# The first attention loads go from GpSimd's DMA queue to SP's

## The chip, the cores and the metric

The kernel runs on one core of one Trainium2 chip. A time is the device time of one execution in microseconds. The engines are TensorE (PE, with its weight loads PEld), VectorE (DVE), ScalarE (ACT), GpSimd (POOL) and SyncE (SP). SP computes nothing; it issues DMAs, and its queue carries nearly all of them. GpSimd computes and issues DMAs too.

## The reference

Two layers of a diffusion backbone over 512 latent tokens and 256 context tokens, width 1024. Each layer is a modulated SwiGLU feed-forward, token mixing, and another feed-forward. Layer 0 mixes by a short convolution and a 2-D Fourier transform, layer 1 by differential attention (8 heads, each with two maps of 64 columns) beside latent attention (8 heads). The part that matters here is the differential head:

```python
s = jnp.einsum('bqhmd,bkhmd->bhmqk', q_da, k_da).astype(f32) * DA_SCALE
p = jax.nn.softmax(s, axis=-1)
w_diff = p[:, :, 0] - lam * p[:, :, 1]
o_da = jnp.einsum('bhqk,bkhd->bqhd', w_diff, v_da.astype(f32))
```

The 512 queries attend to 768 keys (256 of the context, 512 latent) in one softmax.

## The kernel before

All matrix products run in float32r. Where full precision is wanted, a value is split into a high and a low part, and three matmuls are added up (`mm3`, L213 to L215). Weights come in chunks of 512 KB through SP's queue (L129) into three raw buffers; ScalarE makes the high part (L141), VectorE or GpSimd the low part (L143), in four pairs of buffers.

In layer 1 the kernel first makes the projections of the attention. Each result is split into a staging tile (`stg`, four buffers) and stored to DRAM by SP: queries and keys by L727, latent values by L991, values by L845. The order of the last of these items in the program is: keys of head group 0, latent queries (first half), their rotary part, latent queries (second half), values of group 0. The rotary part computes with VectorE (L735), GpSimd (L736, L739) and ScalarE (L738), and stores four times; each half of it gives two stores. The second half of the latent queries gives two more stores. The values of group 0 come in three tiles, with two stores each.

Then the attention begins, as a generator that runs beside the projections of groups 1 to 3, so that TensorE has projection matmuls (keys of group 1 first) between the score matmuls. There are four groups, and each has the heads da 0, mla 0, da 1, mla 1. A head's data is loaded back from DRAM by `load_da` or `load_mla`: for each of the two maps of a differential head the high part of the queries (L1044), the keys (L1045) and the low part of the queries (L1046), and for both maps the values (L1049). The queries are broadcast to both halves of the partitions. All of these are DMAs that GpSimd issues. The first head's loads stand in the program at the start of the attention, behind the value projection of group 0; each later head's stand one query tile after the head before it has begun.

A query tile of a head (`da_unit`) makes scores for map 0 (L1021, four matmuls: high and low queries against 512 and 256 keys), the maximum on VectorE (L1011), the exponential on ScalarE (L1013), and the same for map 1; the difference of the two is then transposed by TensorE (L1030) and multiplied with the values (`av_da`, `st<-wt,v`).

The program's order isn't the order of an engine's queue. A scheduler puts the instructions of each engine in order ahead of the run: what is ready at that point in its own model of time, and among those what comes first in the program. On the chip each engine then takes its instructions strictly in that order, and a DMA that has to wait for a store to land holds up whatever stands behind it on the engine that issues it.

Of the kernel before, what the change touches and what calls it, by code (L numbers as in the profile page):

```python
# [10 lines left out]
F32 = mybir.dt.float32  # L11
# [65 lines left out]
class Builder:  # L77
# [958 lines left out]

    def load_da(self, g, hd):

        dma = self.nc.gpsimd.dma_start
        maps = []  # L1040
        for m in (2 * hd, 2 * hd + 1):
            q, ql, k = self.qstack(), self.qstack(), self.kstack()
            qd = self.qd[g].rearrange("h a r m t -> m h (a r) t")[m]
            dma(out=q, in_=qd[0:1].to_broadcast([2, 64, SEQ]))  # L1044
            dma(out=k, in_=self.kd[g].rearrange("h a r m t -> m (h a r) t")[m])  # L1045
            dma(out=ql, in_=qd[1:2].to_broadcast([2, 64, SEQ]))  # L1046
            maps.append((q, ql, k))
        v = self.atpool.tile([P, 3, 2, 2, P], F32R, name=self.nm("v"), tag="v", bufs=2)
        dma(out=v.rearrange("p j h i c -> p j (h i) c"), in_=self.vd[g][hd])  # L1049
        return maps, v  # L1050
# [606 lines left out]
```

## Time and profile before

| | us |
|---|---|
| median of 3 runs | 2997.54 (2997.32 to 2999.41) |
| the profiled execution | 2996.09 |
| its span | 2994.3 |
| TensorE busy | 2874.3 (96%) |
| VectorE, ScalarE, GpSimd busy | 1650.9, 1043.5, 820.5 |
| the attention's score matmuls, first and last start | 2162.7, 2546.3 |

Every view below counts microseconds from the start of the span. In an order of time, a bracket gives the idle time of the engine before the instruction and what ended it. An issue line gives the tile written, the tile read, the queue, the count, the size of one, and the median time from issue to landing. A releaser named for a wait on several things is the one that came last by the profile. TensorE's granted clock is 1.00 at the higher of its two levels, 2.4 GHz, and 0.50 at the lower, 1.2 GHz.

### The profile page before, as it was taken

The numbers are of one execution on the slowest core, as the hardware profiler recorded it, in microseconds if no ns is written. First come the engines' busy times: TensorE is split into PE (matmuls) and PEld (weight loads), VectorE is DVE, ScalarE is ACT, GpSimd is POOL, SyncE is SP. The second block draws the span as 40 slices with busy tenths as digits, with TensorE's granted clock in tenths as the row PEclk, the third lists the DMA queues.
The fourth block names the chain that finished last, engine by engine and source line by source line (L and its number), as shares of the span: only waits on it lengthen the run. The fifth ranks groups of instructions, "written<-read, shape, count | busy, mean of one in ns | idle before, by whom it ended". The sixth has DMA issues, their size and how long they took to land.

```text
span 2994.3 us, 44211 instructions
## 1 busy us (share of the span) xinstructions
PE 2874.3 (96%) x17842; PEld 2549.9 (85%) x17842; DVE 1650.9 (55%) x2966; ACT 1043.5 (35%) x1733; POOL 820.5 (27%) x441
## 2 busy tenths in 40 slices
PE   6999999999999999999999999999899999999998
PEld 5888888878878888888788888887788888899997
DVE  7866676565475433435845334366366667653335
ACT  4422121444343221124431122244344555552223
POOL 4221112423242111114311111143433332442222
PEclk9999999999999999999999999999999999999999
DMA  7754433323344322233333433352866685452334
GB/s 269 248 166 134 141 135 127 120 86 126 120 142 148 112 85 99 78 120 113 124 130 106 131 116 118 108 167 100 265 166 185 154 211 111 146 175 92 102 103 141
DMA packets 190095, 413.19 MB, mean 138 GB/s; under 512 B 58369, under 2 KB 83585, under 8 KB 189890
## 3 DMA queue, kind: packets, MB, share of 16 engines
q1 hardware_dynamic: 126930, 373.09, 37.6%
q0 software_dynamic: 62960, 37.27, 5.6%
q8 instruction: 140, 2.29, 0.3%
q14 instruction: 65, 0.53, 0.1%
HBM read 375.14 MB, written 35.00 MB: 137 GB/s over the span
## 4 chain that ended last, share of the span: by engine, by line
PE 63%; DVE 6%; DMA 3%; issue 2%; ACT 2%; POOL 2%; SPq 0%; ACTq 0%; POOLq 0%; DVEq 0%
PE mm L213 12%; PE mm L215 12%; PE mm L214 12%; PE pr L214 8%; PE pr L213 8%; PE pr L215 8%; PE pr L1021 2%; PE mm L1030 1%; ACT wh L141 1%; DVE wl L143 1%; DMA ks<-dr 1%; PE st L1115 1%; POOL wl L143 1%; DVE top L1011 1%; DMA dr<-stg 1%
## 5 line engine op out<-in xcount | busy, mean ns | idle before, releaser
L143 POOL TENSOR_TENSOR wl<-wraw,wh 128x1024 fp32r<-128x1024 f32 (+2 forms) x276 | 674.8, 2448 | 1898.1 <-ACT wh L141 1887.5
L141 ACT ACTIVATE wh<-wraw 128x1024 fp32r<-128x1024 f32 (+1 forms) x476 | 494.2, 1039 | 940.7 <-PE mm L214 577.8
L214 PE MATMUL pr<-xm,wh 128*128 128x512 f32 (+1 forms) x1760 | 635.5, 361 | 22.9 <-DVE xm L304 18.1
L213 PE MATMUL pr<-xm,wh 128*128 128x512 f32 (+1 forms) x1760 | 632.3, 360 | 8.3 <-DVE act L221 2.9
L215 PE MATMUL pr<-xm,wl 128*128 128x512 f32 (+1 forms) x1760 | 632.3, 359 | 0.0
L213 PE MATMUL mm<-xm,wh 128*128 128x256 f32 (+1 forms) x1560 | 460.1, 296 | 8.0 <-DVE xm L304 5.0
L215 PE MATMUL mm<-xm,wl 128*128 128x256 f32 (+1 forms) x1560 | 461.5, 296 | 1.8 <-DVE wl L143 1.8
L214 PE MATMUL mm<-xm,wh 128*128 128x256 f32 (+1 forms) x1560 | 460.4, 295 | 0.6 <-DVE xm L304 0.6
L213 PE MATMUL mm<-act,wh 128*128 128x256 f32 (+1 forms) x1408 | 454.1, 324 | 5.9 <-ACT y L504 2.1
L215 PE MATMUL mm<-act,wl 128*128 128x256 f32 (+1 forms) x1408 | 454.0, 323 | 2.6 <-POOL wl L143 2.6
L214 PE MATMUL mm<-act,wh 128*128 128x256 f32 (+1 forms) x1408 | 454.1, 323 | 1.5 <-DVE act L221 1.5
L214 PEld LDWEIGHTS pr<-xm,wh 128*128 128x128 f32 x1760 | 334.6, 190 | 83.5 <-DVE xm L304 27.0
L383 DVE CUSTOM_DVE_ANT_0 junk<-wmod,cond,bmod 128x1024 bf16<-128x1024 f32 x256 | 387.8, 1515 | 9.6 <-DMA wmod<-in_w_mod_dram 6.9
L213 PEld LDWEIGHTS pr<-xm,wh 128*128 128x128 f32 x1760 | 334.5, 190 | 61.4 <-DVE act L221 3.3
L215 PEld LDWEIGHTS pr<-xm,wl 128*128 128x128 f32 x1760 | 334.9, 190 | 51.2
L143 DVE TENSOR_TENSOR wl<-wraw,wh 128x1024 fp32r<-128x1024 f32 x200 | 251.5, 1257 | 210.0 <-ACT wh L141 209.5
L213 PEld LDWEIGHTS mm<-xm,wh 128*128 128x128 f32 x1560 | 295.7, 190 | 18.3 <-DVE xm L304 5.6
L215 PEld LDWEIGHTS mm<-xm,wl 128*128 128x128 f32 x1560 | 295.3, 189 | 10.2 <-DVE wl L143 2.4
L214 PEld LDWEIGHTS mm<-xm,wh 128*128 128x128 f32 x1560 | 295.3, 189 | 8.8 <-DVE xm L304 1.1
L213 PEld LDWEIGHTS mm<-act,wh 128*128 128x128 f32 x1408 | 265.3, 189 | 33.1 <-ACT act L220 3.6
L214 PEld LDWEIGHTS mm<-act,wh 128*128 128x128 f32 x1408 | 266.6, 189 | 26.2 <-DVE act L221 2.7
L215 PEld LDWEIGHTS mm<-act,wl 128*128 128x128 f32 x1408 | 265.8, 189 | 26.8 <-POOL wl L143 3.2
(240 smaller groups left out, 3445.7 us busy)
## 6 DMA issues: line engine op xcount, KB each, us to landing
wraw<-in_w_ffn_in_dram SPq DMA_DIRECT2D x250, 512.0 KB, 3.5
wmod<-in_w_mod_dram SPq DMA_DIRECT2D x160, 512.0 KB, 4.3
wraw<-in_w_ffn_out_dram SPq DMA_DIRECT2D x106, 512.0 KB, 3.6
dr<-stg SPq DMA_DIRECT2D x40, 512.0 KB, 4.7
wraw<-in_w_in_even_dram SPq DMA_DIRECT2D x32, 512.0 KB, 3.5
qs<-dr POOLq DMA_DIRECT2D x56, 256.0 KB, 11.7
dr<-stg SPq DMA_DIRECT2D x36, 256.0 KB, 6.7
ks<-dr POOLq DMA_DIRECT2D x24, 384.0 KB, 11.2
```

Of the source, the lines that this page charges most:

```text
L141: self.nc.scalar.activation(out=h, in_=r, func=AF.Copy)
L143: eng.tensor_tensor(out=l, in0=r, in1=h.bitcast(F32), op=ALU.subtract)
L213: mmul(out, w[0], x[0], start=first, stop=False)
L214: mmul(out, w[0], x[1], start=False, stop=False)
L215: mmul(out, w[1], x[0], start=False, stop=last)
L383: dot = nc.vector.tensor_tensor_reduce(out=junk, in0=w, in1=self.cond[n], op0=ALU.mult, op1=ALU.add, scale=1.0, scalar=self.bmod[:, l, row ...
L1011: nc.vector.tensor_reduce(top, ps, axis=AX.X, op=ALU.max, negate=True)
L1021: self.nc.tensor.matmul(ps[:, c0:c1], q, k[:, c0:c1], start=i == 0, stop=i == len(passes) - 1)
L1030: self.nc.tensor.transpose(ps[:, kt * P:(kt + 1) * P], w[:, (k0 + kt) * P:(k0 + kt + 1) * P], self.ident)
L1115: nc.tensor.matmul(ps, v[:, kt], wt[i][:, :, kt], start=kt == 0 and i == 0, stop=kt == 5 and i == 1)
```

## The change

In `load_da`, for the first head of group 0 alone, the seven DMAs are issued by SP instead of GpSimd. A float32r tile is written through a view as float32, since the source in DRAM is float32. Sizes, buffers and everything else stay.

```diff
     def load_da(self, g, hd):
 
+
         dma = self.nc.gpsimd.dma_start
+        if g == hd == 0:
+            dma = lambda out, in_: self.nc.sync.dma_start(out=out.bitcast(F32), in_=in_)
         maps = []
         for m in (2 * hd, 2 * hd + 1):
             q, ql, k = self.qstack(), self.qstack(), self.kstack()
```

## Rows read from the trace of the kernel before

**Rows 1.** The page of the profile: span, and busy time of TensorE (share, instructions).

```profile
span 2994.3 us, 44211 instructions
...
PE 2874.3 (96%) x17842; PEld 2549.9 (85%) x17842; DVE 1650.9 (55%) x2966; ACT 1043.5 (35%) x1733; POOL 820.5 (27%) x441
```

**Rows 2.** Table by stretch: length; PE, PEld, DVE, ACT, POOL busy; clock; DMA share; GB/s.

```profile
2160.00:2165.00 5.00, 1.04 (x6) 0.54 (x5) 1.01 (x2) 2.09 (x3) 2.50 (x4) 0.81 1.14 347
2165.00:2170.00 5.00, 3.99 (x10) 2.86 (x10) 2.09 (x2) 0.99 (x2) 2.05 (x1) 0.51 1.21 284
2170.00:2175.00 5.00, 4.07 (x19) 3.25 (x19) 2.03 (x4) 0.99 (x2) 0.00 (x0) 1.00 1.10 286
```

**Rows 3.** TensorE in order of time: start, us, instruction, [idle before and releaser].

```profile
2160.28 0.28 PE L215 MATMUL mm<-wh,xm 128*128 128x256 f32 x1
...
2162.70 0.47 PE L1021 MATMUL pr<-ks,qs 128*128 128x512 f32 x1 [2.13 <-DMA wraw<-in_w_da_q_dram]
...
2166.01 1.22 PE L1021 MATMUL pr<-ks,qs 128*128 128x512 f32 x3 [2.83 <-DMA qs<-dr]
...
2171.07 0.74 PE L1021 MATMUL pr<-ks,qs 128*128 128x512 f32 x3 [0.93 <-DMA qs<-dr]
...
2171.64 0.40 PE L213 MATMUL mm<-xm,wh 128*128 128x512 f32 x1
...
2175.14 0.86 PE L1021 MATMUL pr<-ks,qs 128*128 128x512 f32 x4
...
2175.84 0.39 PE L213 MATMUL mm<-xm,wh 128*128 128x512 f32 x1
```

**Rows 4.** GpSimd in order of time, the same columns.

```profile
2145.69 1.28 POOL L736 TENSOR_TENSOR t<-t,t 128x512 f32<-128x512 f32 x1
...
2146.91 0.84 POOL L1044 DMA_DIRECT2D qs<-dr  x1
...
2147.78 1.30 POOL L739 TENSOR_TENSOR stg<-t,stg 128x512 fp32r<-128x512 f32 x1
...
2151.75 0.87 POOL L1046 DMA_DIRECT2D qs<-dr  x1
...
2162.49 0.80 POOL L1059 DMA_DIRECT2D qs<-dr  x1 [9.30 <-DMA dr<-stg]
...
2177.70 0.58 POOL L1049 DMA_DIRECT2D v<-dr  x1 [10.65 <-DMA dr<-stg]
...
2186.01 1.29 POOL L736 TENSOR_TENSOR t<-t,t 128x512 f32<-128x512 f32 x1 [6.87 <-DVE t L735]
```

**Rows 5.** SP's DMA issues in order of time, runs of one kind merged.

```profile
2145.76 7.83 SPq L727 DMA_DIRECT2D dr<-stg  x6
...
2155.14 9.61 SPq L845 DMA_DIRECT2D dr<-stg  x4
...
2167.98 3.15 SPq L845 DMA_DIRECT2D dr<-stg  x2
```

**Rows 6.** DMA from 2140 to 2180: queues; one issue group, median us to landing.

```profile
q1 hardware_dynamic: 6022, 8.34, 64.8%
q0 software_dynamic: 6864, 3.33, 34.7%
...
v<-dr POOLq DMA_DIRECT2D x1, 768.0 KB, 4.4
```

**Rows 7.** Chain of waits, 2155 to 2200: start, us, what.

```profile
2149.59 16.37 DMA qs<-dr
```

**Rows 8.** DMA issues from 2151.6 to 2152, us to landing.

```profile
qs<-dr POOLq DMA_DIRECT2D x1, 256.0 KB, 19.3
```

**Rows 9.** DMA issues from 2145 to 2145.9, us to landing.

```profile
dr<-stg SPq DMA_DIRECT2D x1, 512.0 KB, 3.0
```

**Rows 10.** ScalarE in order of time.

```profile
2159.00 0.60 ACT L220 ACTIVATE stg<-mm 128x512 fp32r<-128x512 f32 x1 [7.37 <-DMA dr<-stg]
```

**Rows 11.** TensorE in order of time, the first product with values.

```profile
2190.58 0.28 PE L213 MATMUL st<-wt,v 128*128 128x256 f32 x1
```

## The prediction

> **What bounds the kernel now.** I read the page first: the span is 2994.3 us and TensorE is busy for 96% of it [rows 1], so the time is TensorE's work plus its gaps, and what a change at one place is worth is read from the gaps there. Next I looked for the place in a table by stretch: between 2160 and 2170 us TensorE is busy for 1.04 and 3.99 us of two stretches of 5, and the granted clock, 1.00 elsewhere, falls to 0.81 and 0.51 [rows 2]. This is the start of the attention, where the moved loads are wanted.
>
> Then TensorE's own order of time [rows 3]. The value projection of head group 0 starts its last matmul at 2160.28; its 256 columns at 2.4 GHz are 0.11 us, so TensorE could go on at about 2160.40. What stands next in its order are the scores of the first query tile. Their first matmul starts at 2162.70, the next ones at 2166.01, those of the second map at 2171.07, and from 2171.64 on the row is dense again. Between 2160.40 and 2171.64 (11.24 us) it does two groups of four score matmuls and six projection matmuls. At full clock a group of four takes 0.70 us (2175.14 to 2175.84) and a projection matmul 0.233 (fifteen from 2171.64 to 2175.14, 3.50 us): 2 x 0.70 + 6 x 0.233 = 2.80 us. So 11.24 - 2.80 = 8.4 us are lost here, the matmuls at the lower clock included.
>
> The cause is the loads. GpSimd issues the six of queries and keys from 2146.91 to 2152.6 [rows 4]. The chain of waits holds the third of them (low part of map 0's queries) for 16.37 us, from 2149.59 to 2165.96, when the scores go on [rows 7]; the sixth, issued at 2151.75, takes 19.3 us [rows 8], to 2171.05, when the second map starts. From 2140 to 2180 the 16 DMA engines have nothing free: the hardware queue takes 64.8% and the software queue 34.7% of them [rows 6].
>
> **The change part by part.** Seven DMAs (2 x query high, key, query low; 1 x value) go from GpSimd's queue to SP's, for group 0's first head alone. Nothing else is edited. The view of the queries as F32 changes no byte.
>
> (a) *GpSimd's issuing goes.* From the first to the end of the sixth are 5.7 us, less 1.3 for an L739 between them: 4.4 us [rows 4]. I count them as nothing: behind them GpSimd waits until 2162.49 for a store to land before it issues the next head's queries, so the time is hidden by that wait. The seventh, the value load, makes GpSimd wait until 2177.70 for the stores of the values; its next work starts at 2186.01 [rows 4], so nothing there either.
>
> (b) *When the loads are issued.* A moved DMA stands in SP's order, which is not the program's: on GpSimd the first load stands before the L739 instruction at 2147.78 that makes the second half of the rotary latent queries, and after the L736 at 2145.69 that belongs to the same half [rows 4], though in the program it comes after both, and after the value projection. So loads are taken as soon as they are held to be ready, at this point. On SP it lies between the stores of the first half and those of the second. SP issues six such stores from 2145.76 to 2153.59 [rows 5]. I take that place; the latest that I hold likely is right behind all six.
>
> (c) *When they land.* At 2146 the queue is short: the store issued at 2145.76 lands in 3.0 us [rows 9]. The software queue moved 3.33 MB in 34.7% of 40 us (240 GB/s at a full share), the hardware queue 8.34 MB in 64.8% (322 GB/s) [rows 6]. The six loads are 4 x 0.256 + 2 x 0.384 = 1.8 MB, 5.6 us at 322 GB/s. The store that lands in 3.0 us needs 1.6 of them for its 0.5 MB, so 1.4 us are its start and end. Behind two stores (3.3 us from 2145.8) the six are moved by 2154.7 and landed by about 2156. Behind all six stores (four more, 2.1 MB, 6.5 us from 2149.1) map 0 (0.9 MB, 2.8 us) would be there at about 2159.8 and map 1 at 2162.6. Map 0 is wanted at 2160.40 and map 1 some 2 us later, after four score and six projection matmuls. So the whole 8.4 us is open to be gained, and about 7.5 at the late place.
>
> A rule of the Trainium skill speaks against this (DMA: Bandwidth & Descriptors, section Queues, rings and completion order): each DMA engine takes turns between the rings that have work, packet by packet, so that on GpSimd's ring the loads have turns of their own, and on SP's they stand behind each store ahead. By that rule they would be slower in landing wherever more than a few stores stand ahead; at the place of (b) the trace sets only 1 MB there, and the sum stays.
>
> (d) *What comes later in exchange.* The other stores stand behind the loads now. The second value tile's evacuation waits 7.37 us on ScalarE until 2159.00 for such a store [rows 10]. The bytes up to there are the same and 1.8 MB of them move faster, so I put these landings within 2 us of now. The PSUM buffers that they hold are wanted by TensorE only some microseconds later. Cost 0, at most 2 us.
>
> (e) *The value load adds a wait to SP.* It can only go when the six value stores have landed. The last two are issued from 2167.98 to 2171.13 [rows 5], and GpSimd, which waits for the same, starts the load at 2177.70; it lands after 4.4 us [rows 6], at 2182.1. Behind it on SP then stand a weight load that nobody needs soon and the next stores, of the keys that TensorE projects in this very stretch. The first matmul that reads these values starts at 2190.58 [rows 11]; 8.4 us earlier that is 2182.2. The slack of 8.5 us is used up almost to the point: I charge 1 us, from 0 up to 5 if the value stores slip with the rest.
>
> Sum: -8.4 + 0 (d) + 1 (e) = -7.4 us, and I take -7, for the small slips that (c) and (d) leave. Later gaps of TensorE hang on its own progress (scores, softmax, transposes), so the gain moves through to the end. The profiled execution took 2996.09 us around its span of 2994.3; minus 7 that is 2989.1. The median of the runs shown is 1.45 us higher, so the forecast for the median is 2990.5. The ends of the unknown costs: -8.4 with another 2 us won by a freer DMA, about 2987; with 2 for (d) and 5 for (e) it is -1.4, about 2996.
>
> **The rivals.**
> *Given back at the values.* The gap goes, but SP's queue is longer by seven DMAs, the value stores slip by 4 to 6 us, and the value load, last in that queue, lands at 2186 to 2188 in place of 2182. TensorE then waits 4 to 6 us at its first product with values, and keeps 2 to 4 us of the gain: 2994.5. For it: SP takes 1.5 to 3 us for an issue when the queue is full (2155.14 to 2171.13 holds six value stores, one weight load and its waits [rows 5]). Against it: that time is the queue's backlog of bytes, and the bytes are no more than now.
>
> *The DMA engines are full, so nothing is won.* The Trainium skill says on the same page (section SWDGE vs HWDGE vs iDMA) that queues of different issuing engines end on the same 16 DMA engines and that another issuer saves only its issuing time. As a mechanism here: the 99.5% in [rows 6] stays, the loads land at 2163 to 2171 as now, and only GpSimd's 5 us goes, which is hidden: 2997.5. Against it: the loads are only 1.8 of 11.7 MB in these 40 us, so it is their place in line that counts, and the hardware queue moves them a third faster. I keep these two together, as they end at no measurable change.
>
> *Slower: the loads stand behind the value stores.* In the program they come after them. If SP's order keeps that, they can go only after 2171.13, when the last value store is issued [rows 5]. At 322 GB/s, behind the 0.5 MB of the last two stores, map 0 would land at about 2171.1 + 1.6 + 2.8 + 1.4 = 2176.9 and map 1 at 2179.7, against 2166 and 2171 now: 9 to 11 us later, and 1 us for more matmuls at the lower clock: 3008. It decides at one point: whether the loads' issues stand before or after the first value store (2155.14). For it: SP is busier than GpSimd, and a store earlier in the program goes first where both are ready. Against it: GpSimd's order held them ready 8 us before that store.
>
> **How the numbers follow.** The forecast gets 0.55 (its own range 2987 to 2993.5), no measurable change 0.27, slower 0.18. About 0.2%, 6 us, is what a measurement of this kernel can tell from no change; the bound is 2991.5. Of the forecast's 0.55 some 0.08 lies short of it, so faster is 0.47, the same 0.35, slower 0.18. The range of 2986 to 3002 leaves out 0.06 below and 0.13 of the slower case.
>
> **What would show it.** Right: between 2160 and 2172 TensorE has no gap over 1 us and the clock stays at 1.00; SP issues the six loads between 2146 and 2154, and they land in under 10 us; the software queue's share of 2140 to 2180 falls from 34.7% to about 15%, which leaves mainly the second head's loads. Step (e): the value load stands on SP behind the last value stores, and the first product with values starts at about 2183. Wrong: loads after 2155 on SP, a wait of the first product with values of over 3 us, or a dense stretch there whose gain is gone before the attention ends at about 2560, which would mean that the order of the later work was set by something other than TensorE.

## The result, and the profile after

The changed kernel takes 3018.68 us (median of 5 runs, 3010.09 to 3024.66) against 2997.32 of the kernel before (5 runs, 2993.23 to 2999.41): ratio 1.0074, 95% interval 1.0059 to 1.0090. It is slower by 21 us where 7 us less were forecast. The profiled execution is the slowest of the five, 3024.66 us.

The page of the changed kernel answers to [rows 1]; the last two lines are its DMA queues (packets, MB, share of 16 engines):

```profile
span 3022.9 us, 44217 instructions
...
PE 2887.3 (96%) x17842; PEld 2560.1 (85%) x17842; DVE 1650.4 (55%) x2966; ACT 1042.5 (34%) x1733; POOL 816.4 (27%) x434
...
q1 hardware_dynamic: 127882, 375.72, 37.6%
q0 software_dynamic: 58368, 34.64, 5.2%
```

The seven loads are 2.6 MB that went from the software to the hardware queue. The table by stretch, as in [rows 2] (the attention's start lies 11 us later in this execution):

```profile
2175.00:2180.00 5.00, 2.21 (x5) 1.49 (x5) 0.00 (x1) 0.00 (x0) 2.51 (x4) 0.50 0.92 191
2180.00:2185.00 5.00, 0.26 (x1) 0.00 (x0) 0.00 (x0) 0.00 (x0) 0.00 (x0) 0.50 0.73 134
2185.00:2190.00 5.00, 0.00 (x0) 0.00 (x0) 0.00 (x0) 0.00 (x0) 0.00 (x0) 0.50 0.42 120
2190.00:2200.00 10.00, 4.77 (x11) 3.41 (x12) 0.96 (x1) 0.99 (x2) 0.00 (x0) 0.50 0.59 182
```

TensorE does 7.2 us of work in 25, at the lower clock, and the other engines all but stand too. Its order of time, which answers to [rows 3]: the value projection ends at 2171.8, and the scores come at 2177.79, 2192.18 and 2199.01, each when a load has landed (for the first the bracket names none; the first key load, issued at 2167.84, takes 9.5 us).

```profile
2171.54 0.28 PE L215 MATMUL mm<-wh,xm 128*128 128x256 f32 x1
...
2177.79 0.76 PE L1021 MATMUL pr<-ks,qs 128*128 128x512 f32 x1 [5.98 <-issue]
...
2192.18 1.22 PE L1021 MATMUL pr<-ks,qs 128*128 128x512 f32 x3 [11.92 <-DMA qs<-dr]
...
2199.01 0.80 PE L1021 MATMUL pr<-ks,qs 128*128 128x512 f32 x1 [3.04 <-DMA ks<-dr]
```

SP's issues, which answer to [rows 5]:

```profile
2157.02 6.35 SPq L727 DMA_DIRECT2D dr<-stg  x6
2163.46 1.20 SPq L129 DMA_DIRECT2D wraw<-in_w_da_q_dram  x1
2164.75 1.91 SPq L845 DMA_DIRECT2D dr<-stg  x2
2166.75 1.04 SPq L1042 DMA_DIRECT2D qs<-dr  x1
2167.84 1.30 SPq L1042 DMA_DIRECT2D ks<-dr  x1
2169.24 1.34 SPq L845 DMA_DIRECT2D dr<-stg  x2
2170.64 6.79 SPq L1042 DMA_DIRECT2D qs<-dr  x2
2177.47 10.29 SPq L1042 DMA_DIRECT2D ks<-dr  x1
2187.86 0.52 SPq L129 DMA_DIRECT2D wraw<-in_w_da_q_dram  x1
2188.49 3.91 SPq L845 DMA_DIRECT2D dr<-stg  x2
2192.49 4.43 SPq L129 DMA_DIRECT2D wraw<-in_w_da_k_dram  x1
2196.97 0.50 SPq L1042 DMA_DIRECT2D qs<-dr  x1
2202.43 0.34 SPq L1042 DMA_DIRECT2D v<-dr  x1
```

Two things stand here that the prediction didn't have. The loads come after all six stores, after a weight load and after the first value tile's stores, and they are strewn among the rest: the last query load stands behind two more weight loads. And SP is held for 6.79 us by two query loads and 10.29 us by one key load. The chain of waits (the low part of map 0's queries takes from 2170.64 to 2192.14, that of map 1's from 2196.97 to 2210.29) answers to [rows 7]:

```profile
2170.64 21.50 DMA qs<-dr
...
2196.97 13.32 DMA qs<-dr
```

From 2207 to 2209 only that last load is moving (packets and MB of these 2 us, then the hardware queue's share of the 16 engines):

```profile
DMA packets 50, 0.10 MB, mean 51 GB/s; under 512 B 0, under 2 KB 0, under 8 KB 50
...
q1 hardware_dynamic: 50, 0.10, 13.2%
```

With nothing beside it, it runs at 51 GB/s on 13.2% of the engines, and 0.132 x 16 = 2.1: it has two engines of sixteen. In the middle of the gap it does not even have these to itself. GpSimd has issued the second head's loads from 2173.86 to 2177.51, and from 2184 to 2187 SP's queue is down to half of that share while most engines stand idle:

```profile
q0 software_dynamic: 132, 0.12, 15.6%
q1 hardware_dynamic: 34, 0.07, 6.9%
```

The two engines are the second cause to be tested; the place in the order is the first.

### The profile page after: what moved, and what is told of

Read it like the earlier page. It is cut to its first block, busy times and chain, and to the rows that moved or that the text cites. A ratio compares the mean times of both kernels' runs of the same rounds, so it can differ in the third digit from the quotient of the medians.

```text
span 3022.9 us, 44217 instructions
## 1 busy us (share of the span) xinstructions
PE 2887.3 (96%) x17842; PEld 2560.1 (85%) x17842; DVE 1650.4 (55%) x2966; ACT 1042.5 (34%) x1733; POOL 816.4 (27%) x434
## 4 chain that ended last, share of the span: by engine, by line
PE 64%; DVE 5%; DMA 3%; ACT 2%; issue 2%; POOL 1%; SPq 0%; ACTq 0%; DVEq 0%; POOLq 0%
PE mm L213 12%; PE mm L215 12%; PE mm L214 12%; PE pr L214 8%; PE pr L213 8%; PE pr L215 7%; PE pr L1021 2%; DMA qs<-dr 1%; PE mm L1030 1%; ACT wh L141 1%; PE st L1118 1%; POOL wl L143 1%; DMA ks<-dr 1%; DVE wl L143 1%; DVE top L1011 1%
## 5 line engine op out<-in xcount | busy, mean ns | idle before, releaser
L215 PEld LDWEIGHTS mm<-xm,wl 128*128 128x128 f32 x1560 | 295.9, 190 | 11.4 <-DVE wl L143 3.6
```

Source lines behind the costliest of these rows:

```text
L215: mmul(out, w[1], x[0], start=False, stop=last)
```

## The experiments

Totals of one kernel spread by 13 to 32 us between runs here (the kernel before: 2983 to 3015 in 29 runs of the first set), so each profile was also measured on the stretch alone: from the start of TensorE's 11,600th matmul to that of its 12,400th, the last value projection and the start of the attention. All kernels have 17,842 matmuls. The table gives this stretch in us, from one profile each.

```
kernel                         median (before beside it)  ratio, 95% interval       stretch
before                         2997.32                                               130.1
e12 before again               2995.44, one run                                      129.8
changed                        3018.68 (2997.32)          1.0074 (1.0059 to 1.0090)  152.1
e1  changed again              3024.53 (2997.57)          1.0083 (1.0051 to 1.0115)  152.8
e2  halves                     3008.80 (2997.57)          1.0032 (1.0012 to 1.0053)  137.0
e3  early                      3011.04 (2997.57)          1.0032 (1.0013 to 1.0051)  140.3
e4  early and halves           2993.11 (2997.57)          0.9981 (0.9960 to 1.0002)  123.1
e5  queries only on SP         3018.63 (2998.73)          1.0063 (1.0044 to 1.0081)  152.3
e6  keys and values only       3002.75 (2998.73)          1.0005 (0.9987 to 1.0022)  136.1
e7  halves on GpSimd           2989.85 (2998.73)          0.9972 (0.9949 to 0.9994)  122.8
e8  ScalarE's queue            3018.09 (2998.73)          1.0056 (1.0036 to 1.0076)  152.3
e9  leading 2, no copy         3007.09 (2998.36)          1.0025 (1.0005 to 1.0044)  138.9
e10 all halves, GpSimd         2985.46 (2998.36)          0.9954 (0.9938 to 0.9970)  124.5
e11 all halves, first early    2986.21 (2998.36)          0.9962 (0.9951 to 0.9973)  122.3
```

**e1, e12: the kernels again.**

> The changed kernel itself, timed beside the three kernels of this set. Two theories of the 21 us. WIDTH: a query load is written as a broadcast, its access pattern has the two copies as the outermost dimension, and on SP's hardware queue such a DMA runs on 2 of the 16 DMA engines (the slices of the changed profile that hold nothing else show a DMA share of 0.13 to 0.14 and 45 to 55 GB/s, which is two engines' worth), so 256 KB take at least 5 us, four such loads 20 us, and SP itself is held while those two rings are full. PLACE: the loads stand in SP's order among and behind the value stores and two weight loads, and this place alone makes them late. Both expect the measured time again, 3010 to 3025 us, with TensorE's gap of some 23 us net at the start of the attention.

> The kernel before, unchanged, for a second profile. The runs are compared by the stretch from the 11,600th to the 12,400th TensorE matmul (the last value projection and the attention's start), which was 130.1 us in the first profile of the kernel before and 152.1 and 152.8 in two of the changed kernel. Every theory that puts the loss into this stretch expects 129 to 131.5 again. If it is 135 or more, the stretch varies by itself and the differences of single profiles (7 us down in the halves runs) prove less.

Both as expected: 152.8 and 152.1 against 129.8 and 130.1. The stretch repeats within 0.8 us, and it holds the whole loss (22 to 23 us).

**e2: halves.** Each query load of the first head becomes two DMAs of 64 partitions (shortened; the low part likewise, and the other heads' loads stay).

```diff
-            dma(out=q, in_=qd[0:1].to_broadcast([2, 64, SEQ]))
+            for c in (slice(0, 64), slice(64, 128)):   # first head only
+                dma(out=q[c], in_=qd[0])
```

> The changed kernel, with each query load of the first head written as two DMAs of 64 partitions each (the same bytes, no broadcast), on SP as before; the place in SP's order stays much the same (first pair behind the first value tile's stores, map 1 even behind the second weight load). WIDTH: the loads run on 16 engines, land in under 8 us each, no slice of 0.13 is left, and the time is 2993 to 3002 us, the rest of the loss being the place. PLACE: the order is no better than in the changed kernel, so the time stays at 3010 to 3025.

Neither range was met: 3008.80 is between them. The stretch gives back 15 of the 22 us; 7 stay lost. So the width is most of it, and there is something beside it.

**e3: early.** The scheduler gets the first head's loads with priority.

```diff
+            if i == 0:
+                with self.tc.high_priority(2000):
+                    loads[heads[i]] = self.load_da(g, hd)
+                return
```

> The changed kernel, with the first head's loads given priority, so that they stand in SP's order between the first of the rotary part's stores and the rest of them, ahead of all value stores (the place that the prediction assumed); still broadcasts. WIDTH: four query loads of 5 us or more on the same two engines take 20 us from about 2147 on, the second map's low part lands at about 2168 to 2172, and the stores behind them are held; the time is 2996 to 3010. PLACE: the loads land before 2160 and the time is 2987 to 2993.

It is just above WIDTH's range (3011.04, 1 us over its end). The place alone gives back 12 us of the stretch and doesn't save the change. SP's order now is that of step (b): one store, then all six loads, then the other five.

```profile
2159.23 5.11 SPq L1042 DMA_DIRECT2D qs<-dr  x2
2164.39 5.66 SPq L1042 DMA_DIRECT2D ks<-dr  x1
2170.10 0.55 SPq L1042 DMA_DIRECT2D qs<-dr  x1
2170.69 10.93 SPq L727 DMA_DIRECT2D dr<-stg  x5
```

The scores hardly wait any more (1.2 us). What TensorE waits for is a buffer in PSUM, the memory it writes its results to: 13.3 us before one projection matmul, since the evacuations (the copies out of PSUM) wait for staging tiles whose stores stand behind the narrow loads. Its wait row (total, times, longest):

```profile
PE mm L213 <- DVE stg L221: 13.7, 2, 13.3
```

**e4: early and halves**, both edits.

> Both edits: loads ahead of all value stores in SP's order, and query loads as two DMAs of 64 partitions. WIDTH and PLACE together expect what the prediction expected of the change: the loads land within 10 us, no TensorE gap over 1 us between 2160 and 2172, 2987 to 2993 us. If the time is 2995 or more, something else that the prediction left out is lost at this place (the stores behind the loads, or the value load).

2993.11, 0.1 us above the range. The interval just touches no change, so the total alone shows no gain; the stretch does, with 123.1, 6.7 to 7.0 us under the kernel before. SP issues all loads between 2147.65 and 2153.7, in 0.3 to 0.6 us a DMA, and the value load at 2177.33:

```profile
2147.65 1.10 SPq L1042 DMA_DIRECT2D qs<-dr  x2
2148.81 0.57 SPq L1042 DMA_DIRECT2D ks<-dr  x1
2149.42 2.36 SPq L1042 DMA_DIRECT2D qs<-dr  x4
2151.83 0.63 SPq L1042 DMA_DIRECT2D ks<-dr  x1
2152.50 1.24 SPq L1042 DMA_DIRECT2D qs<-dr  x2
2154.78 4.28 SPq L727 DMA_DIRECT2D dr<-stg  x5
...
2177.33 0.33 SPq L1042 DMA_DIRECT2D v<-dr  x1
```

Around these scores TensorE has no gap over 0.5 us and keeps the higher clock (1.00); map 1 follows map 0 after 2.8 us, and the first product with values doesn't wait for them (rows as in [rows 3] and [rows 11]):

```profile
2161.64 0.85 PE L1021 MATMUL pr<-ks,qs 128*128 128x512 f32 x4
2164.45 0.86 PE L1021 MATMUL pr<-ks,qs 128*128 128x512 f32 x4
...
2185.34 0.28 PE L213 MATMUL st<-wt,v 128*128 128x256 f32 x1
```

**e5, e6: the change by parts.** Only the lines of the queries, or only those of keys and values, go through SP.

> Of the seven loads only the four query loads (broadcasts) go on SP's queue; keys and values stay with GpSimd. In SP's order the first two stand behind the first value tile's stores, the other two behind the second's. WIDTH: these four are what costs; 1 MB on two engines is some 20 us from about 2156 on (the shift of the early part left out), the last lands at 2176 to 2182, and the loss is 8 to 20 us: 3005 to 3018. If it were the place alone, the loss would be smaller than that of the halves run (11 us), since here none stands behind a weight load: 2998 to 3005.

> Only the two key loads and the value load go on SP's queue (128 rows outermost, all 16 engines); the query loads stay with GpSimd as broadcasts. WIDTH: no slice of 0.13, no SP issue of over 4 us; the keys come 5 to 10 us earlier than on GpSimd or not at all later, and the time is that of the kernel before, 2990 to 3002. PLACE: the keys stand behind two and four value stores, so the scores wait for them: 3003 to 3012.

The four query loads alone make the whole loss (152.3 in the stretch; 3018.63, 0.6 us above WIDTH's range). Keys and values cost nothing that the totals show, but 6 us in the stretch (a profile of the slowest of ten runs): the keys stand behind value stores, and the first scores come after a gap of 9.1 us. There PLACE was partly right, and my WIDTH range (up to 3002) was missed by 0.75.

**e8: ScalarE's queue** (shortened).

```diff
-            dma = lambda out, in_: self.nc.sync.dma_start(...)
+            dma = lambda out, in_: self.nc.scalar.dma_start(...)
```

> The seven loads as broadcasts on ScalarE's hardware queue, a ring of their own, so that nothing of SP's is ahead or behind; they stand ahead of the value evacuations in ScalarE's order. WIDTH: still two engines per query load, 20 us for four of them, with ScalarE held in its issues of 5 us or more, which delays the evacuation of the values: 3000 to 3020. PLACE: free of SP's order the loads land by 2160: 2988 to 2995.

As WIDTH expected. A hardware queue of their own, with the loads started at 2151, doesn't help: by the times of their packets the query loads never keep more than 2.1 engines busy. Now ScalarE is held in its issues and idle for 18.7 us:

```profile
2152.89 8.76 ACTq L1042 DMA_DIRECT2D qs<-dr  x2
2161.68 10.31 ACTq L1042 DMA_DIRECT2D ks<-dr  x1
2172.12 0.60 ACT L220 ACTIVATE stg<-mm 128x512 fp32r<-128x512 f32 x1 [18.70 <-issue]
```

**e9: why narrow.** The edit of e4, and a gap between the two rotary halves in DRAM (the loads that read around it are left out here).

```diff
-            dst = self.qd[g] = self.dram([2, 2, 32, 4, SEQ])
+            dst = self.qd[g] = self.dram([2, 2, 33 if g == 0 else 32, 4, SEQ])[:, :, :32]
```

> The early-halves kernel, with a gap of one row put between the two rotary halves of group 0's queries in DRAM (33 rows for 32), so that a load of 64 partitions reads 2 x 32 x 512 and its outermost dimension is 2, though nothing is read or written twice. The order on SP is the same. It tells apart why a query load is narrow: if the OUTERMOST DIMENSION sets the number of DMA engines, the eight half loads run on two engines, slices of 0.13 DMA share come back, and the start of the attention is about as slow as in the early run (17 us slower than early halves there): 3003 to 3014. If reading the same DRAM rows twice (the BROADCAST itself) was slow, this is as fast as early halves: 2987 to 2996.

The outermost dimension it is. Half loads that copy nothing twice, but read 2 x 32 x 512, bring the loss of the early run back (138.9 against 140.3, and 123.1 without the gap). From 2170 to 2172 only they move, at 51 GB/s and 13.2% again; four of them hold SP for 8.33 us, where the four of e4 take 2.36, and TensorE waits for the same PSUM buffer.

```profile
2155.94 8.33 SPq L1042 DMA_DIRECT2D qs<-dr  x4
```

```profile
PE mm L213 <- DVE stg L221: 13.2, 1, 13.2
```

**e7: the control on GpSimd**, the edit of e2 without the change.

> Control: the kernel before (all loads on GpSimd), with the first head's query loads as two DMAs of 64 partitions each. If the software queue spreads a broadcast over all 16 engines, as the steady 1.0 share of the stretch suggests, nothing is won, four more issues of 0.8 us come on GpSimd, and the time is 2994 to 3002. If it too is confined to two engines, the loads land 5 us or more earlier and the time is 2988 to 2993.

The first branch of the expectation (nothing won) was wrong and the second holds: 2989.85, and 7 us of the stretch. So these loads are narrow on the software queue too, and the kernel before shows it. From 2193 to 2195 one query load of a later head (issued at 2190.52) moves 50 packets of 2,048 B, the only ones of that size: 51 GB/s. From 2221 to 2224 two more (issued at 2214.22 and 2215.57), with what is left of a third load that is no broadcast, are all that moves, at about twice that:

```profile
DMA packets 152, 0.30 MB, mean 101 GB/s; under 512 B 4, under 2 KB 4, under 8 KB 152
q0 software_dynamic: 152, 0.30, 35.4%
```

As broadcasts (kernel before) these two land in 10.6 us, as halves (e10, below) in 4.9:

```profile
qs<-dr POOLq DMA_DIRECT2D x2, 256.0 KB, 10.6
qs<-dr POOLq DMA_DIRECT2D x4, 128.0 KB, 4.9
```

The queues differ in what several such loads do together. Here they add up: two have about 100 GB/s, and from 2351 to 2354, where only broadcasts have packets of 2,048 B, 168 of these make 115. On SP's queue two share the 51: in e5 the last two query loads are issued by 2177.97, and from 2180 to 2190 their 254 packets of 2,048 B move at 52 GB/s. So the move put onto two engines, one behind the other, what had run side by side.

A broadcast on the software queue has small packets besides. The pages of the kernel before, e7 and e10 count:

```profile
DMA packets 190095, 413.19 MB, mean 138 GB/s; under 512 B 58369, under 2 KB 83585, under 8 KB 189890
DMA packets 186575, 413.18 MB, mean 138 GB/s; under 512 B 54849, under 2 KB 80065, under 8 KB 186370
DMA packets 147856, 413.02 MB, mean 138 GB/s; under 512 B 16130, under 2 KB 41346, under 8 KB 147651
```

From the first to the second 3,520 packets go, 880 for each of the four loads, all of them under 512 B (4 B each in the trace); the data packets stay 2,048 B. How much of the 7 us is theirs and how much is the width's was not tried.

**e10, e11: all broadcasts as halves**, without and with the first head early on SP.

> The kernel before, with all query loads that were broadcasts (both kinds of heads, all groups) as two DMAs of 64 partitions each, on GpSimd. The control with the first head alone gained 7 us at the attention's start. If the software queue's small packets were also what later heads wait for, a few us more come: 2984 to 2990. If later loads are early enough anyway, it stays at 2987 to 2993; 44 more issues on GpSimd (0.55 us for a half against 0.83 for a broadcast, some 0.3 us each pair) are hidden.

> All query loads as halves; the first head's on SP ahead of the value stores, the others on GpSimd. The two gains at the attention's start are for the same gap, so they do not add: 2984 to 2992, within 4 us of the run with all halves on GpSimd.

Both within their ranges and better than both kernels: 2985.46 and 2986.21, ratios 0.9954 and 0.9962. In e10 all 48 broadcasts are halves, and 880 small packets go for each of them (third line above). The move to SP adds nothing to it that can be measured.

## Why the prediction was wrong, step by step

What bounds the kernel was read rightly: the gap at the attention's start is the loads', and filling it is worth what was worked out. (8.4 less 1 us for the values gave -7.4; e4 and e7, which fill it in two ways, measure -6.7 to -7.3 in the stretch.) What failed is the claim that this change fills it.

(a) GpSimd's issuing was hidden, as said: its next loads come at 2173.86, 11.4 us later than before, in an execution that is 11.2 us behind there.

(b) *The place, wrong.* I took from GpSimd's order the time at which the loads are held ready, and set it into SP's order at the same place. The planner's order for SP put them after the first value stores, the point at which the slower rival was said to decide. e3 and e4 put them where (b) had them, and win 13 us (without halves, 3024.53 to 3011.04) and 16 us (with, 3008.80 to 2993.11).

(c) *The rate, wrong by six, and by the stretch the slightly larger step.* The hardware queue's 322 GB/s was taken from weights and stores, whose outermost dimension is 128 partitions; a query load with 2 copies outermost has 51 GB/s, and two at once share it. The software queue's 240 GB/s was such a mean too, and hid that the loads were narrow there already. The four loads need 4 x 5.1 = 20 us on the same two engines, not 1.05 MB at 322 GB/s, 3.3 us, and longer where the second head's loads take half of these engines. SP, in order, is held behind them (that what it feeds is full is my reading; no view shows it), so the keys, the value stores and the weights wait as well. Halves win 16 us at the late place and 18 at the early one (15 and 17 in the stretch, where the place wins 12 and 14; the totals don't tell the two steps apart). The Trainium skill states just this (DMA: Bandwidth & Descriptors, section Rules for kernel authors): an outermost dimension smaller than 16, a leading broadcast for instance, confines a DMA to at most as many engines as it has entries. The runs agree for SP's and ScalarE's queues (2.1 engines; e9 without a broadcast), and GpSimd's has the same 51 GB/s a load. The prediction weighed two other rules of that page and not this one, the only one that looks at the shape of the moved load.

(d) Right with wide loads (e4 waits 0.8 us for such a buffer), wrong with narrow ones: 13.3 us in e3. Its bound of 2 us rested on the rate of (c).

(e) Right where it can be seen: in e4 the value load is issued at 2177.33, against 2177.70 in the prediction, and lands 6.4 us later, in time for 2185.34. In the changed kernel it doesn't matter.

The slower rival (3008) named the right mechanism of the order, but with loads at full rate: e2, the run nearest to it, measures 3008.8. That they agree so closely is luck in part, since e2's loads stand behind two to six of the value stores and the rival's behind all six. The further 10 to 16 us are the width, which no rival had. The rival of full DMA engines fell: e4 moves the same bytes and wins the gap, and in the changed kernel the engines' share falls to 0.42 from 2185 to 2190 and to 13% from 2206, while everything waits for two of them.

Left open: by its 11,600th matmul the first profile of the changed kernel is 11.2 us behind the kernel before, in instructions whose order is the same. It isn't the change: over all fourteen profiles that matmul starts between 2127.5 and 2139.1, at 2127.5 in e5, which moves four of the loads, and in the second profile of the kernel before 4.8 us later than in the first. What makes this spread wasn't tried.

## What to carry to other kernels

Before a load goes to another queue, look at its access pattern and not only at its bytes. In these runs the outermost dimension decided how many DMA engines worked on a load, and on SP's or ScalarE's queue all loads with 2 outermost shared two of 16 and held up everything that was issued behind them. Write such a load as one DMA for each copy. For the first head's four loads that won 0.28% on the old queue, no less than together with the move and the early place (0.19%, an interval that touches no change); for all 48 it won 0.5%. And a DMA's place in another engine's in-order queue has to be read from that engine's order; it doesn't come along with the move.

## What the runs showed of the hardware that was not expected

A load with 2 outermost moves at 51 GB/s, 2.1 engines by their busy share on SP's queue, whether it reads rows twice (changed kernel) or not (e9); on ScalarE's queue it never keeps more than 2.1 busy (e8), and on the software queue one by itself has 51 GB/s as well. Two at once share the 51 on SP's queue (e5), while on the software queue several have up to 115 together (kernel before). Behind narrow loads the issuing engine itself is held: 10.29 us for SP in one issue of a key load that takes 0.63 in e4, and 18.7 us without work for ScalarE. On the software queue a broadcast has 880 packets of 4 B more for each 256 KB load than its two halves.
